# A list scheduler in the kernel sets the order of all five engines in the first mixer of a two-layer decoder trunk

## The chip, the cores and the metric

The kernel runs on one core of a Trainium2 chip. A core has five engines with queues of their own: TensorE (PE in the profile, PEld for its loads of weights), VectorE (DVE), ScalarE (ACT), GpSimd (POOL) and SyncE (SP), which here only starts transfers. Each engine works through its instructions in the order in which the program holds them; semaphores make it wait for the others. The metric is the device time of one execution in microseconds (us), as the median of several runs.

## The reference

The input x has 256 tokens of 2048 channels in fp32. Two layers follow, each a mixer, a gated FFN with a convolution, and a small embedding term. Only the mixer of the first layer, a gated DeltaNet, is touched here:

```python
def gdn_mixer(x, w_in, conv_w, a_log, dt_bias, norm_g, w_o):
    proj = x @ w_in                                   # 2048 -> q 2048, k 2048, v 4096, z 4096, a 32, b 32
    ...
    qkv = silu(causal_dwconv(qkv, conv_w))            # 4 taps along the tokens
    q = l2norm(q) * 128 ** -0.5; k = l2norm(k)        # 16 heads of 128, each used by two of 32 value heads
    beta = sigmoid(b)
    g = -exp(a_log) * softplus(a + dt_bias)
    o = gated_delta_rule(q, k, v, g, beta)
    o = o * rsqrt(mean(o ** 2) + eps) * norm_g * silu(z)
    return o @ w_o                                    # 4096 -> 2048

def gated_delta_rule(q, k, v, g, beta):               # per head; the reference takes chunks of 64 tokens
    ...
    lmat = where(strict, (k * beta) @ k.T * decay, 0)
    sol = triangular_solve(lmat + I, [v * beta, k * beta * exp(gc)])
    ...                                               # scan over chunks: v_new, o_n, state S

x = layer_norm(ALPHA * x + gdn_mixer(x, ...))
```

## The kernel before

**Products.** Every fp32 weight block is 512 KB: SP loads it into a `raw` tile (line 99), ACT writes its upper part `hi` (L103), DVE the rest `lo` = raw − hi (L104); three buffers each. x is kept transposed and split in the same way (`xT`). PE takes x·hi and x·lo in a fast fp32 form. `gemm_t` gives transposed results, 256 columns at a time in two PSUM tiles `mm_ps`: a block is 8 products of 512 columns (L124) and 8 of 256 (L128). `gemm` gives rows, in two tiles `b_ps`: 8 products with hi (L148, L149) and 4 with lo (L152). These PSUM tiles share four buffers (`mm`). The small products of the mixer are plain fp32 and use two buffers `sp` and two buffers `bk`.

**Stages of the mixer.** The 32 value heads are taken as eight groups of four; a group uses two key heads. For each group: keys `k` and queries `q` (256 columns each), values `v` and gates `zs` (512 each), all from `w_in`; keys, queries and values pass through a fold of the two halves of `mm_ps` (L184 on ACT, L185, the join, on DVE), four taps and a tanh. `lower` makes the 256x256 triangle `L` of each head as two diagonal blocks, `l_ps` (L465) by the decay (rows `qd` loaded from the DRAM tile `grow`, L450) by `c` (L472). 32x32 blocks of L go through DRAM (`lt`, then `ld`) to `substitution`, 31 steps on DVE that invert them for four groups at once (`xi`), and back through DRAM (`tt`) into `pm`, which has one buffer (L510, on POOL). `inverses` makes `W` from L and pm (`w_ps`). `front` prepares the decayed score tiles `qd`, `qo`, `n21`. `solve` runs two halves, each pm·rhs and then three products with W, with DVE or ACT between any two (`s_ps`, L504). `outputs` takes `o_ps` (L607, L608), squares (ACT), a reciprocal root on DVE, the scaled tile `ot` (L620), its transposes `ot_ps` (L624) and the split result `oT` (L626, L627). `mixed` multiplies oT of two groups (kt = 8) with w_o and adds to x (L224, L226); the last group's part is done by the following stage (`project`).

**What sets the order.** Emission order by hand in `gdn_groups`, and a scheduler of the framework that places instructions by priority when their operands should be ready. Two devices of the kernel act on it: `hi` and `lo` are emitted with raised priority, and `weights` draws one or two substitution steps per block from the generator `self.aside`. Small products may land anywhere, also in the middle of a block.

Of the kernel before, what the change touches and what calls it, by code (L numbers as in the profile page):

```python
# [57 lines left out]

class Trunk:
    def __init__(self, nc, tc, ctx, t):  # L60
# [21 lines left out]
        self.aside, self.share = iter(()), 0  # L82
# [10 lines left out]
    def weights(self, src, rows, nk, cols):  # L93
# [13 lines left out]
        for _ in range(self.share):  # L107
            next(self.aside, None)
# [196 lines left out]
    def gdn_gates(self, pool, w, gk):  # L305
        nc, t = self.nc, self.t
        ab, dt, al, gr = w[:64, 0:S], w[:, 256:288], w[:, 288:320], w[:64, 320:448]
        self.gemm_t(t["gdn_w_in"], 12288, 64, self.xT, lambda n, ps: self.fold(pool, ab, ps))
        nc.scalar.activation(al, al, AF.Exp)
        ps = self.sp.tile([P, 2, 64], F32, tag="sp", name="ab_ps")  # L310
        for a in range(2):
            nc.tensor.transpose(ps[:, a], ab[:, a * P:(a + 1) * P], self.ident[:64, :64])

        x, e, s, s2, q, g = (
            w[:, o:o + 64].rearrange("p (a h) -> p a h", a=2) for o in range(448, 832, 64))
        nc.vector.tensor_tensor(x, ps[:, :, 0:32], bcast(dt, 2, 1), op=ALU.add)
        nc.vector.scalar_tensor_tensor(e, x, -1.0, x, op0=ALU.mult, op1=ALU.max)
        nc.scalar.activation(e, e, AF.Exp, scale=-1.0)
        nc.vector.tensor_scalar(s, e, 2.0, None, op0=ALU.add)
        nc.vector.reciprocal(s, s)  # L320
        nc.vector.tensor_tensor(s, s, e, op=ALU.mult)
        nc.vector.tensor_tensor(s2, s, s, op=ALU.mult)
        nc.vector.tensor_scalar(q, s2, 1.0 / 17, None, op0=ALU.mult)
        for m in (15, 13, 11, 9, 7, 5, 3):
            nc.vector.scalar_tensor_tensor(q, q, 1.0 / m, s2, op0=ALU.add, op1=ALU.mult)
        nc.vector.scalar_tensor_tensor(q, q, 1.0, s, op0=ALU.add, op1=ALU.mult)
        nc.vector.tensor_scalar(x, x, 0.0, None, op0=ALU.max)
        nc.vector.scalar_tensor_tensor(x, q, 2.0, x, op0=ALU.mult, op1=ALU.add)
        nc.vector.scalar_tensor_tensor(g, x, -1.0, bcast(al, 2, 1), op0=ALU.mult, op1=ALU.mult)

        self.beta = gk.tile([P, 2, 32], F32, tag="beta", name="beta")
        nc.scalar.activation(self.beta, ps[:, :, 32:64], AF.Exp, scale=-1.0)
        nc.vector.tensor_scalar(self.beta, self.beta, 1.0, None, op0=ALU.add)
        nc.vector.reciprocal(self.beta, self.beta)

        self.gc = gk.tile([P, 2, 32], F32, tag="gc", name="gc")
        self.gout = gk.tile([P, 32], F32, tag="go", name="go")
        g64 = g.rearrange("p a h -> p (a h)")
        pc = self.sp.tile([P, 256], F32, tag="sp", name="gc_ps")
        nc.tensor.matmul(pc[:, 0:64], self.tri, g64, start=True, stop=True)  # L340
        nc.tensor.matmul(pc[:, 64:96], self.ones, g[:, 0], start=True, stop=True)
        nc.tensor.matmul(pc[:64, 128:256], g64, self.tri, start=True, stop=True)
        nc.vector.tensor_copy(self.gc.rearrange("p a h -> p (a h)"), pc[:, 0:64])
        self.ngc = gk.tile([P, 2, 32], F32, tag="ngc", name="ngc")
        nc.vector.tensor_scalar(self.ngc, self.gc, -1.0, None, op0=ALU.mult)
        nc.vector.tensor_tensor(self.gout, pc[:, 64:96], self.gc[:, 0], op=ALU.subtract)
        nc.vector.tensor_copy(gr, pc[:64, 128:256])
        self.grow = self.dr.tile([64, P], F32, tag="grow", name="grow", bufs=1)
        nc.gpsimd.dma_start(out=self.grow, in_=gr)

    def gdn(self):
        nc, tc, t = self.nc, self.tc, self.t
        self.op = tc.alloc_tile_pool(name="op", bufs=2)
        with tc.tile_pool(name="gk", bufs=1) as gk, tc.tile_pool(name="gw", bufs=1) as pool:
            cw = gk.tile([P, 4, 64], F32, tag="cw", name="cw")
            ng = gk.tile([P, 1], F32, tag="ng", name="ng")
            cr = pool.tile([64, 4, P], F32, tag="v", name="cr")
            w = pool.tile([P, 1024], F32, tag="xi", name="gates")
            for i, k in enumerate(("gdn_dt_bias", "gdn_a_log")):
                nc.gpsimd.dma_start(out=w[:, 256 + 32 * i:288 + 32 * i],  # L360
                                    in_=bass.AP(tensor=t[k].tensor, offset=t[k].offset, ap=[[0, P], [1, 32]]))
            nc.gpsimd.dma_start(out=cr, in_=t["gdn_conv_w"].rearrange("k (n c) -> n k c", c=P))
            nc.gpsimd.dma_start(out=self.cst, in_=t["cst"][:, P:])
            nc.gpsimd.dma_start(out=ng, in_=t["gdn_norm_g"].rearrange("(p o) -> p o", o=1))
            nc.gpsimd.tensor_scalar(ng, ng, 0.5, None, op0=ALU.mult)

            def load(nb):
                cs = slice(nb * 512, (nb + 1) * 512)
                for a in range(2):
                    nc.sync.dma_start(out=self.x[:, a, cs], in_=t["x"][a * P:(a + 1) * P, cs])  # L370
                for a in range(2):
                    self.to_xT(self.xT, self.x[:, a, cs], a, nb * 4)
                if nb == 2:
                    ps = self.sp.tile([P, 4, 64], F32, tag="sp", name="cw_ps")
                    for k in range(4):
                        nc.tensor.transpose(ps[:, k], cr[:, k], self.ident[:64, :64])
                    nc.vector.tensor_copy(cw, ps)

            self.gdn_groups(pool, gk, cw, ng, load, lambda: self.gdn_gates(pool, w, gk))

    def gdn_groups(self, pool, gk, cw, ng, load, gates):
# [277 lines left out]
        for g in range(8):  # L659
# [13 lines left out]
            if g == 7:  # L673
                mixed(6, 1)
# [311 lines left out]
```

## Time and profile before

| | us |
|---|---|
| median of three runs | 2897.72 |
| the three runs | 2894.42, 2897.72, 2898.40 |
| the profiled execution | 2893.65 |
| its span | 2891.7 |
| its first mixer, up to the projection's first products | 916 |

The profiled execution is a run of its own, 4.1 us under the median; rows of the profile are compared with its time. Its mean granted clock of TensorE is 0.995 of full speed. In the views that follow, a row names a line of the kernel, the engine, and a tile and what it is made from; numbers in brackets behind a row say how long the engine had been idle and what released it. A view by windows gives the busy time of each engine in a stretch, with the number of instructions in round brackets.

### The profile page before, as it was taken

The page shows a single profiled execution, that of the slowest core. Times are in us where ns is not written, and L with a number is a line of the kernel's source. Part 1 is how long each engine was busy: PE and PEld are TensorE (multiplying, and loading weights), DVE is VectorE, ACT ScalarE, POOL GpSimd, SP SyncE. Part 2 cuts the span into 40 slices and gives each one's busy share as a digit, 9 for nine tenths or more (in the row PEclk, how much of TensorE's full clock was granted, in tenths as well). Part 3 has the DMA queues.
Part 4 walks back from the last instruction along what each step waited for, and adds up shares of the span by engine and source line. Part 5 has one row for each costly group of instructions (what it writes and reads, how often), then busy time and mean ns, then how long its engine had stood idle before and what let it go on. Part 6 is the DMA issues. An engine that isn't in the chain of part 4 may idle for free. (4 is left out here: it accounts for less than half of the span.)

```text
span 2891.7 us, 40953 instructions
## 1 busy us (share of the span) xinstructions
PE 2825.3 (98%) x15654; PEld 2432.9 (84%) x15654; DVE 1864.7 (64%) x3007; ACT 1427.1 (49%) x2259; POOL 115.0 (4%) x192
## 2 busy tenths in 40 slices
PE   8999999999999999999999999999999999999998
PEld 6888787788887888888888878888888888888887
DVE  6886668766666766666554665766576666654465
ACT  4755536544543655455433543455365555543353
POOL 0100000000000000000000000110000000000000
PEclk9999999999999999999999999999999999999999
DMA  6665555455554566666655556554556666655555
GB/s 190 197 182 150 153 156 177 148 155 155 164 156 139 168 201 203 193 210 200 199 192 190 186 178 201 172 161 134 194 168 196 194 194 194 195 192 190 193 189 179
DMA packets 415077, 519.70 MB, mean 180 GB/s; under 512 B 19708, under 2 KB 313984, under 8 KB 414880
## 3 DMA queue, kind: packets, MB, share of 16 engines
q1 hardware_dynamic: 407136, 496.76, 54.6%
q0 software_dynamic: 7744, 20.32, 2.9%
q8 instruction: 123, 2.02, 0.3%
q14 instruction: 74, 0.61, 0.1%
HBM read 512.76 MB, written 7.39 MB: 180 GB/s over the span
## 5 line engine op out<-in xcount | busy, mean ns | idle before, releaser
L104 DVE TENSOR_TENSOR lo<-raw,hi 128x1024 fp32r<-128x1024 f32 x925 | 1131.7, 1225 | 791.7 <-ACT hi L103 761.0
L103 ACT ACTIVATE hi<-raw 128x1024 fp32r<-128x1024 f32 x925 | 977.2, 1057 | 1273.0 <-PE b_ps L149 533.6
L124 PE MATMUL mm_ps<-xT,hi 128*128 128x512 f32 (+1 forms) x4176 | 1068.4, 396 | 13.4 <-ACT qd L531 4.7
L124 PEld LDWEIGHTS mm_ps<-xT,hi 128*128 128x128 f32 (+1 forms) x4176 | 750.8, 189 | 148.8 <-ACT qd L531 4.9
L128 PEld LDWEIGHTS mm_ps<-xT,lo 128*128 128x128 f32 (+1 forms) x4176 | 574.0, 190 | 39.9
L128 PE MATMUL mm_ps<-xT,lo 128*128 128x256 f32 (+1 forms) x4176 | 600.1, 284 | 0.0
L148 PE MATMUL b_ps<-hi,xT 128*128 128x512 f32 (+2 forms) x736 | 274.7, 379 | 2.9 <-ACT sg L786 1.7
L149 PE MATMUL b_ps<-hi,xT 128*128 128x512 f32 (+2 forms) x736 | 274.3, 379 | 0.0
L148 PE MATMUL b_ps<-hi,hTA 128*128 128x512 f32 (+1 forms) x640 | 212.4, 347 | 0.0
L149 PE MATMUL b_ps<-hi,hTA 128*128 128x512 f32 (+1 forms) x640 | 212.3, 347 | 0.0
L152 PE MATMUL b_ps<-lo,xT 128*128 128x512 f32 (+2 forms) x736 | 195.7, 383 | 1.9 <-DVE lo L104 1.9
L148 PEld LDWEIGHTS b_ps<-hi,xT 128*128 128x128 f32 x736 | 139.0, 189 | 29.5 <-ACT sg L786 3.0
L149 PEld LDWEIGHTS b_ps<-hi,xT 128*128 128x128 f32 x736 | 139.3, 190 | 24.7
L152 PEld LDWEIGHTS b_ps<-lo,xT 128*128 128x128 f32 x736 | 130.8, 189 | 25.1 <-DVE lo L104 2.8
L152 PE MATMUL b_ps<-lo,hTA 128*128 128x512 f32 (+1 forms) x640 | 138.6, 347 | 0.0
L149 PEld LDWEIGHTS b_ps<-hi,hTA 128*128 128x128 f32 x640 | 121.2, 189 | 15.0
L148 PEld LDWEIGHTS b_ps<-hi,hTA 128*128 128x128 f32 x640 | 121.2, 189 | 14.9
L152 PEld LDWEIGHTS b_ps<-lo,hTA 128*128 128x128 f32 x640 | 105.1, 189 | 15.0
L148 PE MATMUL b_ps<-hi,oT 128*128 128x512 f32 (+1 forms) x264 | 101.7, 389 | 0.0
L149 PE MATMUL b_ps<-hi,oT 128*128 128x512 f32 (+1 forms) x264 | 101.4, 386 | 0.0
L408 DVE SCALAR_TENSOR_TENSOR ac<-pd,cw,ac 128x256 f32<-128x256 f32 x192 | 86.3, 479 | 4.6 <-ACT ac L406 4.2
L725 DVE SCALAR_TENSOR_TENSOR fac<-fpd,fcw,fac 128x256 f32<-128x256 f32 x160 | 77.3, 483 | 12.9 <-ACT fac L723 10.0
(265 smaller groups left out, 2351.5 us busy)
## 6 DMA issues: line engine op xcount, KB each, us to landing
raw<-in_gdn_w_in SPq DMA_DIRECT2D x193, 512.0 KB, 3.8
raw<-in_ffn_w_gate SPq DMA_DIRECT2D x160, 512.0 KB, 4.6
raw<-in_ffn_w_up SPq DMA_DIRECT2D x160, 512.0 KB, 4.2
raw<-in_ffn_w_down SPq DMA_DIRECT2D x160, 512.0 KB, 3.6
raw<-in_dsa_w_in SPq DMA_DIRECT2D x80, 512.0 KB, 3.5
raw<-in_gdn_w_o SPq DMA_DIRECT2D x64, 512.0 KB, 3.6
raw<-in_ple_w_gate SPq DMA_DIRECT2D x64, 512.0 KB, 3.7
raw<-in_dsa_w_o SPq DMA_DIRECT2D x32, 512.0 KB, 3.5
```

The lines of the kernel that those rows point to most:

```text
L103: nc.scalar.activation(hi, raw, AF.Copy)
L104: ins = nc.vector.tensor_tensor(lo, raw, hi.bitcast(F32), op=ALU.subtract)
L124: nc.tensor.matmul(q[:m, :], hi[:, k, o:o + m], x[:, k0 + k].rearrange("p a b -> p (a b)"), start=k0 + k == 0, stop=False)
L128: nc.tensor.matmul(q[:m, S:], lo[:, k, o:o + m], x[:, k0 + k, 0, :], start=False, stop=k0 + k == kt - 1)
L148: nc.tensor.matmul(ps[a][:, :n], xh, hi[:, k, :], start=k0 + k == 0, stop=False)
L149: nc.tensor.matmul(ps[a][:, :n], xl, hi[:, k, :], start=False, stop=False)
L152: self.last = nc.tensor.matmul(ps[a][:, :n], x(k0 + k)[:, 0, a * P:(a + 1) * P], lo[:, k, :], start=False, stop=k0 + k == kt - 1)
L408: nc.vector.scalar_tensor_tensor(ac, pd[:, k:k + S], w[:, k:k + 1], ac, op0=ALU.mult, op1=ALU.add)
L725: nc.vector.scalar_tensor_tensor(ac, pd[:, k:k + S], cw[:, k, n:n + 1], ac, op0=ALU.mult, op1=ALU.add)
```

## The change

The mixer is written as tasks, each with an engine, a duration in us (a constant in the code), an emitting function, tasks that come before it, and the buffers it takes and gives back (`raw`, `mm`, `sp`, `qd`, `pm`, ...). `Plan.run` simulates the five engines and the transfers with these numbers, picks at each step the task that can start first (among those that could start now, the lowest rank), and emits it. The whole is put into the program under a manual schedule for all five engines, so the framework's scheduler no longer moves anything there. The blocks of weights have a fixed order on PE (`run`, `merge`); every small product is a task between two half blocks. The rest of the program is unchanged, except that in this stage's last blocks the projection's first hi and lo are mixed in.

```diff
+class Plan:
+    LAG = {"PE": 0.6, "DVE": 0.25, "ACT": 0.25, "POOL": 0.2, "SP": 0.2}
...
+    def run(self):
+        while True:
+            best = None
+            for engine, tasks in self.open.items():
+                pick, at = None, self.at[engine]
+                for t in tasks:
+                    s = self.start(t)
+                    if s is None:
+                        continue
+                    key = (s if s > at + 0.05 else 0.0, t.rank(), t.order)
+                    if pick is None or key < pick[0]:
+                        pick = key, s, t
+                if pick and (best is None or pick[1] < best[1]):
+                    best = pick
...
+            self.at[t.engine] = s + t.cost
+            t.end = s + t.cost + t.tail
...
+            for n in t.then:
+                n.left -= 1
+                n.ready = max(n.ready, t.end + (n.lag if n.engine != t.engine or t.tail else 0.0))
...
+            with tc.manual_schedule(engines=engines):
+                self.gdn_plan(pool, gk)
...
+        plan = self.plan = Plan(raw=3, hi=3, lo=3, mm=4, sp=2, bk=2, fold=2, pd=2, ac=2, k=6, q=1, v=2, vt=1, zs=2, oT=2,
+                                qd=2, qo=2, n21=2, sq=1, L=5, pm=1, W=1, u=1, y0=1, y=2, wq=2)
...
+            urgent = lambda: 0 if i <= plan.now + 1 else 3
...
+            d = add(Q, 0.38, load, take=["raw"], rank=i, bus=2.2, tail=1.8)
+            h = add(A, 1.06, high, [d], take=["hi"], rank=urgent)
+            l = add(V, 1.23, low, [h], take=["lo"], give=["raw"], rank=urgent)
...
+            p = add(E, b["cost"][0], lambda: product(0), deps, take=["mm"] * 2 * b["first"], rank=5, lag=0.1)
+            p = b["task"] = add(E, b["cost"][1], lambda: product(1), [l, p], give=["hi", "lo"], rank=4, lag=0.1)
...
+            d = add(Q, 0.4, lambda: rows_into(g, tile()), [rows["go"]], take=[take], rank=lambda: plan.now + 2.5, bus=2.2, tail=3.5)
...
+                    p = add(V, 0.69, lambda scale=scale: scale((0, 1)), [p, dec[g][a], d], rank=5 if b else 3)
...
+                d = add(V, 0.36 + 0.0028 * m * n, step, [d, z], rank=5 if b else 3.5)
...
+                ld.append(add(G, 0.6, fill, [s["t"], *ld[:1]], take=["pm"] * (not c), tail=3.5))
...
-            lT = pool.tile([P, 32, 32], F32, tag="u", name="lT")
-            nc.vector.tensor_copy(lT, ld.rearrange("p i j -> p j i"))
...
-            if g in (2, 4, 6):
-                mixed(g - 2, 2)
...
+        run([x for y in zip(keys(0), keys(1)) for x in y])
+        run(column(w_in, 0, 12288, 64, KT, lambda k: self.xT[:, k], True, None, decay_gates))
+        run(keys(2))
+        run(keys(3))
+        batch(0)
+        run(gates(0))
+        run(merge(queries(0) + values(0), gates(1)))
...
+        for g in range(1, 7):
+            c = queries(1) if g == 1 else []
+            c = c + values(g)
+            if g < 3:
+                c = c + keys(2 * g + 2) + keys(2 * g + 3)
+            if g == 6:
+                c = c + values(7)
+            c = c + queries(g + 1)
+            z = gates(g + 1)
+            if g < 6:
+                z = z + mixes(g - 1)
+            run(merge(c, z))
...
+        run(mixes(5))
+        run(mixes(6))
+        plan.run()
```

Work that differs: `mixes` takes one group at a time (kt = 4), so x is added to 56 times in place of 32; L is scaled inside its own tile, which the decay rows are loaded into; the substitution reads `ld` with a stride in place of a transposed copy; `outputs` writes over `zs` in place of `ot`; the sums of squares of the keys go through four small instructions per batch in place of one. The numbers of products on PE and of transfers are the same.

The first place is DVE while the first four groups' L are scaled (`L<-l_ps,c,L`); `pd<-mm_ps,fold` is the join that frees a PSUM tile of the wide products. Before:

```order
L104 TENSOR_TENSOR lo<-raw,hi 128x1024
L472 SCALAR_TENSOR_TENSOR L<-l_ps,c,L 128x128 x8
L104 TENSOR_TENSOR lo<-raw,hi 128x1024
L472 SCALAR_TENSOR_TENSOR L<-l_ps,c,L 128x128 x7
L104 TENSOR_TENSOR lo<-raw,hi 128x1024
L472 SCALAR_TENSOR_TENSOR L<-l_ps,c,L 128x128 x6
L104 TENSOR_TENSOR lo<-raw,hi 128x1024
L472 SCALAR_TENSOR_TENSOR L<-l_ps,c,L 128x128 x6
L185 TENSOR_TENSOR pd_109<-mm_ps,fold 128x256
L185 TENSOR_TENSOR pd_110<-mm_ps,fold 128x256
```

The same place after (L515 is lo, L845 the scaling, L548 the join, L623 the swish of the z gate):

```order
L845 SCALAR_TENSOR_TENSOR L<-l_ps,c,L 128x128 x6
L515 TENSOR_TENSOR lo<-raw,hi 128x1024
L623 SCALAR_TENSOR_TENSOR zs<-zs,b_ps 128x512
L845 SCALAR_TENSOR_TENSOR L<-l_ps,c,L 128x128 x2
L515 TENSOR_TENSOR lo<-raw,hi 128x1024
L623 SCALAR_TENSOR_TENSOR zs<-zs,b_ps 128x512
L845 SCALAR_TENSOR_TENSOR L<-l_ps,c,L 128x128 x2
L515 TENSOR_TENSOR lo<-raw,hi 128x1024
L845 SCALAR_TENSOR_TENSOR L<-l_ps,c,L 128x128 x2
L515 TENSOR_TENSOR lo<-raw,hi 128x1024
L845 SCALAR_TENSOR_TENSOR L<-l_ps,c,L 128x128 x4
L515 TENSOR_TENSOR lo<-raw,hi 128x1024
```

Scalings stand in runs of 6 to 8 between two lo before, and in runs of 2 to 6 after; the z gate, which needs no join, is done here, and the next joins (`pd`) come after the last scaling and one more lo.

The second place is the end of the mixer on DVE: the last reciprocal root `rs`, the scaled outputs of the last group, and their split transposes `oT`. Before:

```order
L251 SCALAR_TENSOR_TENSOR rs_8261<-rt_8262,rs_8261 128x8
L620 SCALAR_TENSOR_TENSOR ot<-o_ps,rs_8261,zs 128x128 x8
L627 SCALAR_TENSOR_TENSOR oT<-ot_ps,ng,oT 128x4x128 x2
L104 TENSOR_TENSOR lo<-raw,hi 128x1024 x2
L224 TENSOR_TENSOR x<-x,b_ps 128x512
```

And after (L1045 is the scaling, L303 a residual addition, L185 a lo of the projection, L1061 the split):

```order
L1045 SCALAR_TENSOR_TENSOR zs<-o_ps,rs_8235,zs 128x128 x2
L515 TENSOR_TENSOR lo<-raw,hi 128x1024
L303 TENSOR_TENSOR x<-x,b_ps 128x512 x2
L515 TENSOR_TENSOR lo<-raw,hi 128x1024
L1045 SCALAR_TENSOR_TENSOR zs<-o_ps,rs_8235,zs 128x128 x4
L515 TENSOR_TENSOR lo<-raw,hi 128x1024
L303 TENSOR_TENSOR x<-x,b_ps 128x512
L185 TENSOR_TENSOR lo<-raw,hi 128x1024
L303 TENSOR_TENSOR x<-x,b_ps 128x512
L1045 SCALAR_TENSOR_TENSOR zs<-o_ps,rs_8235,zs 128x128 x2
L185 TENSOR_TENSOR lo<-raw,hi 128x1024
L1061 SCALAR_TENSOR_TENSOR oT<-ot_ps,ng,oT 128x4x128
```

Before, the eight scalings and the two splits follow each other with no weights between; now five lo and the additions of other blocks stand among them.

The third place is PE in the first groups' solve: wide products (`mm_ps`) and small ones (`s_ps`, `w_ps`, `ss_ps`). Before:

```order
L124 MATMUL mm_ps<-xT,hi 128x512 x2
L504 MATMUL s_ps<-vt,pm 128x128
L124 MATMUL mm_ps<-xT,hi 128x512 x5
L504 MATMUL s_ps<-vt,pm 128x128
L124 MATMUL mm_ps<-xT,hi 128x512
L504 MATMUL s_ps<-vt,pm 128x128 x2
L128 MATMUL mm_ps<-xT,lo 128x256 x8
L124 MATMUL mm_ps<-xT,hi 128x512
L504 MATMUL s_ps<-y_2228,W 128x128 x4
L124 MATMUL mm_ps<-xT,hi 128x512 x4
L504 MATMUL s_ps<-y,W 128x128 x4
L124 MATMUL mm_ps<-xT,hi 128x512 x3
```

After (L478 and L475 are the wide products with hi and lo, L916 the small products of the solve, L772 sums of squares):

```order
L478 MATMUL mm_ps<-xT,hi 128x512 x8
L916 MATMUL w_ps<-pm,L 128x96 x8
L475 MATMUL mm_ps<-xT,lo 128x256 x8
L916 MATMUL s_ps<-vt,pm 128x128 x4
L478 MATMUL mm_ps<-xT,hi 128x512 x8
L772 MATMUL ss_ps<-cst,sq 128x1 x4
L916 MATMUL s_ps<-y_1960,W 128x128 x4
L475 MATMUL mm_ps<-xT,lo 128x256 x8
```

Small products split half blocks before; after, they stand whole between two halves.

More of the change, by code (lines that the diff above doesn't have):

```diff
@@ L302, in layer_norm @@
         return affine
[L305 to L349, printed above, removed]
@@ L359, in gdn @@
[L359 to L364, printed above, removed]
@@ L365, in gdn @@
[L365 to L377, printed above, removed]
@@ new lines, in mixes, with done @@
+        def mixes(g):
+            r = []
+            for nb in range(4):
+                c = nb * 512
+                def done(state, task, c=c, nb=nb):
+                    for a in range(2):
+                        add(V, 0.69, lambda a=a: self.residual(self.x[:, a, c:c + 512], state["ps"][a], None,
+                                                               1.0 if g else ALPHA),
+                            [task], give=["mm"] + ["oT"] * (nb == 3 and a), rank=1)
+                r += column(t["gdn_w_o"], 4 * g * P, c, 512, 4, lambda k: O[g]()[:, k], False, lambda k0: od[g], done)
+            return r
@@ new lines, in merge, with run @@
+        def merge(a, b):
+            pairs = [b[i:i + 2] for i in range(0, len(b), 2)]
+            n, j, r = len(a) // 4, 0, []
+            for i in range(n):
+                k = len(pairs) * (i + 1) // n
+                mine, j = pairs[j:k], k
+                mid = mine[:1] if len(mine) > 1 else []
+                r += a[4 * i:4 * i + 2] + sum(mid, []) + a[4 * i + 2:4 * i + 4] + sum(mine[len(mid):], [])
+            return r
+        def run(blocks):
+            for b in blocks:
+                place(b)
@@ new lines, in squares, with sq, product @@
+        def squares(y, deps, use, take=()):
+            box = {}
+            def sq():
+                box["sq"] = new("sq", [2, S])
+                nc.scalar.activation(box["sq"], y(), AF.Square)
+            def product():
+                ps = box["ps"] = sps("sp", [4], "ss_ps")
+                for h in range(2):
+                    for a in range(2):
+                        nc.tensor.matmul(ps[:, 2 * h + a:][:, 0:1], box["sq"][:, h, a * P:(a + 1) * P],
+                                         self.ones[:, 0:1], start=True, stop=True)
+            d = add(A, 0.63, sq, deps, take=["sq"], rank=3)
+            d = add(E, 0.7, product, [d], take=["sp"], give=["sq"], rank=1)
+            return add(V, 0.17, lambda: use(box["ps"]), [d], take=take, give=["sp"], rank=2)
@@ new lines, in gdn_plan, with taps @@
+        add(Q, 0.4, lambda: None, bus=0.6)
+        tb0 = {}
+        def taps():
+            ps = tb0["ps"] = sps("sp", [4, 64], "cw_ps")
+            for k in range(4):
+                nc.tensor.transpose(ps[:, k], cr[:, k], self.ident[:64, :64])
+        quarter(0)
+        tapped = add(E, 0.3, taps, [there], take=["sp"], rank=1)
+        tapped = add(V, 0.4, lambda: nc.vector.tensor_copy(cw, tb0["ps"]), [tapped], give=["sp", "u"], rank=1)
+        for nb in range(1, 4):
+            quarter(nb)
@@ L677, in gdn_groups @@
             if g == 1:
[L678 to L679 removed]
+                front(1)
             if g == 2:
[L681 to L683 removed]
+                batch(1)
+            group(g)
+            front(g + 1)
+        group(7)
+        run(mixes(5))
+        run(mixes(6))
+        plan.run()
+        self.heads[7] = O[7]()
     def project(self, pool, src, h, kt, g, b, prepare, side=1, scale=ALPHA):
```

807 lines of the change are left out of this document (556 added, 251 removed).

## The prediction

> **What bounds the kernel now.** I read the first page of the profile, then a table by stage, then what PE waits for in the first mixer, then the timeline around the longest of those waits.
>
> ```profile
> span 2891.7 us, 40953 instructions
> PE 2825.3 (98%) x15654; PEld 2432.9 (84%) x15654; DVE 1864.7 (64%) x3007; ACT 1427.1 (49%) x2259; POOL 115.0 (4%) x192
> ```
>
> PE is busy for 98% of the span and no other engine for more than 64%, apart from the weight loads, which overlap PE. So the time can only fall by less idle PE, a higher granted clock, or less work on PE. The next rows are the first mixer and the stage behind it: microseconds, then busy time and count of PE, PEld, DVE, ACT and POOL, granted clock, DMA share, GB/s.
>
> ```profile
> 0.00:916.00 916.00, 871.47 (x4875) 741.97 (x4875) 638.49 (x1222) 473.84 (x904) 47.43 (x87) 0.99 0.56 164
> 916.00:1740.00 824.00, 817.07 (x4489) 707.18 (x4489) 517.80 (x705) 403.25 (x558) 25.89 (x47) 1.00 0.61 192
> ```
>
> The mixer leaves PE idle for 916.00 − 871.47 = 44.5 us; the next stage, of nearly the same length, for 6.9. All that a better order can win lies in those 44.5 us, in the clock lost behind them, and in what PE itself pays for the order of its products. The waits of PE from the start to 935 us (waiting instruction, releaser, us in total, times, longest):
>
> ```profile
> PE ot_ps L624 <- DVE ot L620: 10.8, 8, 4.5
> PE v_ps L563 <- DVE v L411: 6.3, 3, 5.2
> PE t_ps L195 <- DMA x<-in_x: 5.8, 2, 4.9
> PE mm_ps L124 <- ACT qd L531: 4.7, 1, 4.7
> PE l_ps L465 <- DVE oT L627: 3.3, 2, 2.0
> PE mm_ps L124 <- DVE xT L189: 3.3, 2, 1.8
> PE mm_ps L124 <- ACT hi L103: 2.9, 1, 2.9
> PE t_ps L195 <- DVE xT L189: 1.8, 1, 1.8
> PE s_ps L504 <- DVE y L595: 1.6, 2, 0.9
> PE b_ps L148 <- DVE pd L185: 1.2, 1, 1.2
> PE s_ps L504 <- DVE vt L587: 1.0, 1, 1.0
> PE s_ps L504 <- ACT y L590: 0.7, 1, 0.7
> PE kk_ps L425 <- ACT sq L422: 0.4, 1, 0.4
> ```
>
> They add up to 43.8 us, the idle time of the stage. Three single waits (4.5, 5.2, 4.7) make a third of it. Their causes:
>
> ```profile
> 105.03 1.22 DVE L104 TENSOR_TENSOR lo<-raw,hi 128x1024 fp32r<-128x1024 f32 x1 [1.32 <-ACT hi L103]
> 106.17 1.64 DVE L472 SCALAR_TENSOR_TENSOR L<-l_ps,c,L 128x128 f32<-128x128 f32 x6
> 107.73 0.74 DVE L185 TENSOR_TENSOR pd<-mm_ps,fold 128x256 f32<-128x256 f32 x2
> 108.28 1.19 PE L124 MATMUL mm_ps<-xT,hi 128*128 128x512 f32 x2 [4.72 <-ACT qd L531]
> 457.98 0.69 ACT L528 ACTIVATE qo<-qd,go 128x128 f32<-128x128 f32 x2 [4.35 <-DMA qd<-grow]
> 459.66 1.23 DVE L104 TENSOR_TENSOR lo<-raw,hi 128x1024 fp32r<-128x1024 f32 x1 [3.34 <-ACT hi L103]
> 463.97 1.12 PE L563 MATMUL v_ps<-ident,v 128*128 128x128 f32 x4 [5.15 <-DVE v L411]
> 909.52 0.39 PE L608 MATMUL o_ps<-u,qd 128*128 128x128 f32 x2
> 914.37 0.97 PE L624 MATMUL ot_ps<-ident,ot 128*128 128x128 f32 x3 [4.46 <-DVE ot L620]
> ```
>
> At 108 us the named releaser, ACT's qd, is not the real one. PE needs an mm buffer, and the two DVE joins that free it (L185) begin at 107.73, behind six scalings of L and a weight split that nobody is waiting for yet. At 458 us ACT stands 4.35 us at the head of its queue for a transfer (qd from grow); the next hi half, the convolution and PE follow late. At 914 us PE has nothing left beside the last group: its o_ps products end at about 910, and squares, rsqrt and scaling must pass before the transposes.
>
> **Clock.** The same columns as above, for the stretch behind each of these waits, for a stretch after recovery, and for one with short waits:
>
> ```profile
> 108.20:113.00 4.80, 4.71 (x15) 4.05 (x16) 3.88 (x11) 4.80 (x15) 2.55 (x5) 0.52 0.50 149
> 463.70:469.00 5.30, 5.03 (x17) 4.12 (x17) 3.85 (x8) 3.56 (x9) 0.00 (x0) 0.61 0.72 224
> 914.30:919.00 4.70, 4.63 (x14) 2.81 (x15) 3.32 (x10) 1.37 (x2) 1.02 (x2) 0.64 0.00 0
> 113.00:117.00 4.00, 4.00 (x30) 3.69 (x28) 3.06 (x7) 3.91 (x10) 0.33 (x1) 1.00 0.59 180
> 521.00:527.00 6.00, 4.41 (x29) 3.64 (x27) 3.81 (x8) 1.44 (x2) 0.56 (x1) 1.00 0.73 229
> ```
>
> Each long wait is followed by about five microseconds at a granted clock of 0.52 to 0.64. At 521 to 527 us PE idles 1.6 us in shorter pieces and the clock stays at 1.00.
>
> **The change, part by part.**
>
> *Long waits.* Whatever frees an mm buffer on DVE (join, swish, addition) now carries rank 1 and the scalings of L rank 3; at this place the z gate's blocks run, and their swish stands between short runs of scalings. The decays' rows are loaded by a rank among the weights and their ACT pieces, cut to two heads each, carry rank 4, so hi halves don't stand behind them. In the tail, five blocks of other products stand between the last o_ps and the last transposes; a block lasts 2.80 us by the chain of waits in steady running:
>
> ```profile
> 1773.75 1.84 PE mm_ps L124 x8
> 1776.55 1.84 PE mm_ps L124 x8
> ```
>
> Five blocks are 14.0 us, against the 4.9 us from 909.52 to 914.37 that the chain took. I count all three as gone: 4.72 + 5.15 + 4.46 = −14.3.
>
> *Clock behind them.* 4.8 × 0.48 + 5.3 × 0.39 + 4.7 × 0.36 = 2.3 + 2.1 + 1.7 = −6.1, work that then runs at full speed. The Trainium skill, "TensorE: Matmul & The Clock Gate", section "HAM oscillation — how this bites in real kernels", puts it as half clock for a window of about 3.4 us after any idle gap of that length; the trace agrees on which waits do it, and an estimate from that page, three times 1.7 us, would make this term −5.1 instead.
>
> *Head.* The first x (4.9), the rest of that row (0.9), the first hi (2.9) and the two rows on xT (3.3, 1.8) are 13.8. What waits for the first transfers cannot go: 4.9 + 2.9. The remaining 6.0 hangs on transposes, splits and joins in a queue that is now ordered by rank; I take half, −3.0.
>
> *Other waits.* 43.8 − 14.3 − 13.8 = 15.7, in 17 pieces of at most 2.0 us. The planner sends a dependent task at least 0.6 us after a PE task in its own count, so most should go, but it also makes new places: some 160 groups of small products (v 16, w 8, s 72, o 16, ot 16, l 8, g 8, squares 16) now stand at fixed spots between half blocks, each ready or not by its own jitter. I take 12 us of waits left, old and new: −3.7. Ends: nothing left, −15.7, and more than before (first rival).
>
> *PE's own order.* Small fp32 products no longer split a half block; changes from small to large products fall from 196 to 133. What such a change costs is seen at the starts here:
>
> ```profile
> 892.21 0.40 PE L148 MATMUL b_ps<-hi,oT 128*128 128x512 f32 x1
> 892.44 0.40 PE L149 MATMUL b_ps<-hi,oT 128*128 128x512 f32 x1
> 892.76 1.16 PE L504 MATMUL s_ps<-y,W 128*128 128x128 f32 x8
> ```
>
> From large to large 0.23, from large to small 0.32: 0.09 us more. 63 × 0.09 = −5.7. If the way back costs as much it is −11.3; if the next group swallows it, nothing.
>
> *More additions on DVE.* w_o is now taken one group at a time, which adds 24 residual additions; the two copies that transposed L go, which I count as nothing.
>
> ```profile
> L104 DVE TENSOR_TENSOR lo<-raw,hi 128x1024 fp32r<-128x1024 f32 x252 | 308.4, 1224 | 166.8 <-ACT hi L103 145.3 <-ACT ac L406 6.9 <-ACT y L590 6.5
> L224 DVE TENSOR_TENSOR x<-x,b_ps 128x512 f32<-128x512 f32 x24 | 16.3, 682 | 8.2 <-PE b_ps L152 8.2
> ```
>
> 24 × 0.682 = 16.4 us: DVE goes from 638 to 655 of some 883 us, 74%. They lie beside PE's products: the sum has 0 for them. Covered by DVE's idle time, 167 us of it in front of lo alone. Without that cover each addition would hold an mm buffer for 0.7 us longer; at worst the whole 16.4 comes onto the path. PE's product counts are unchanged, so nothing for those. The small tensor_scalars, four per batch in place of one, are covered likewise.
>
> *Seam.* The loads of the first layer norm's rows on POOL are moved behind other loads that wait for the same last oT, and their use lies tens of microseconds later: 0.
>
> *Sum.* −14.3 − 6.1 − 3.0 − 3.7 − 5.7 = −32.8. The profiled execution took 2893.65 us, so 2860.9 by its account. It lies 4.1 below the median of the three runs before and 0.8 below the fastest; half of the 4.1 added gives **2863**.
>
> **Rivals.**
>
> 1. *The plan has no slack where the chip has jitter.* Every engine runs in a fixed order, and a late transfer or a long DVE piece holds all behind it. For it: ACT's 4.35 us above is such a case. Against it: three raw buffers and 167 us of DVE idling on hi. At 0.1 us for each of 160 groups that is 16 us more waits: −17, so about **2878**.
>
> 2. *Slower: the reload of pm.* It has one buffer, written by four POOL transfers per group, which must wait for the last read of the group before. In the new order the first w_ps of a group stands 2.6 to 3.0 blocks behind that read in five places, so 7.3 to 8.4 us.
>
> ```profile
> L510 POOL DMA_DIRECT2D pm<-tt x32: 582/582/616, 177.2 to 828.6; - x32
> pm<-tt POOLq DMA_DIRECT2D x32, 32.0 KB, 2.4
> ```
>
> Four issues are 4 × 0.58 = 2.3 us, and the landing has a median of 2.4 (last column), so it fits by about 3 us. If landing took 13 us there, each of five waits would be 2.3 + 13 − 7.8 = 7.5 us and cost 2.0 in clock: +47, so **2908**. It decides for slower from 6.6 us each on (32.8 / 5), a landing of about 10 us. Against it: that is four times the median.
>
> 3. *Slower: the clock.* With small groups at every half block PE may idle briefly all the time, and the granted clock could swing without one long wait. At 0.80 over the some 245 us in which solves and outputs run (8 groups × 11 blocks × 2.80), 61 us are lost: **2922**. The 521 us row speaks against it: 1.6 us idle of 6, clock 1.00. The Trainium skill, same page, section "A second HAM failure mode: psum-queue depth-cycling", says that PE idling for a moment between groups of matmuls is enough to make the clock swing; by that rule this rival would come about, and the trace so far does not bear it out.
>
> 4. *No gain.* The waits named above are replaced by others of the same sum and the switches cost nothing: **2897**.
>
> **How the numbers follow.** The forecast, between −25 and −45 (2850 to 2870 with the 2 us for the runs): 0.62. Its lower end is the sum with all middle waits gone, −44.8; its upper end is the sum without the terms for switches and other waits, rounded up. Rival 1, 2870 to 2890: 0.20. No gain: 0.08. Rival 2: 0.06, rival 3: 0.04. What can be told from no change is about 0.2%, 5.8 us, so 2892 to 2903. The range 2850 to 2890 takes the forecast and rival 1, 0.82. Faster 0.82, same 0.08, slower 0.10.
>
> **What would show it.** In the profile after: PE waits of the first mixer of 20 to 25 us in all, with the first x (4.9) the longest; no stretch under 0.9 in granted clock behind the first 20 us; no single wait above 3 us behind the head; the stage's end, the first products of the projection, some 30 us earlier than 916, near 883; DVE busy in the stage up by about 15; the later 1975 us unchanged within a few. Wrong: w_ps waiting for pm on POOL (rival 2), a clock between 0.6 and 0.9 over tens of microseconds in groups (rival 3), many waits of 0.3 to 1 us on s_ps or ss_ps (rival 1). A time below 2850 would mean that switches cost PE both ways.

## The result and the profile after

The changed kernel takes 2851.93 us in the median of four runs (2850.62 to 2857.97); the kernel before, 2896.56 in the median of its four. The ratio is 0.985, 95% interval 0.9833 to 0.9867: 44.6 us or 1.5% less. The forecast was 2863 with 2850 to 2890. The profiled execution of the changed kernel is the slowest of its four, 2857.97 us.

The first page, and the mixer up to the transposes of the next stage's column vectors (`col_ps`), which begin at 928.7 us before and at 888.3 after. The window's columns are microseconds, busy time and count of PE, PEld, DVE, ACT, POOL, granted clock, DMA share, GB/s. Before:

```profile
0.00:928.70 928.70, 884.17 (x4925) 751.45 (x4925) 645.44 (x1230) 478.88 (x909) 52.81 (x99) 0.99 0.55 163
```

After:

```profile
span 2855.9 us, 40967 instructions
PE 2811.6 (98%) x15654; PEld 2438.0 (85%) x15654; DVE 1898.3 (66%) x3035; ACT 1428.2 (50%) x2259; POOL 115.2 (4%) x192
...
0.00:888.30 888.30, 869.28 (x4924) 755.16 (x4924) 678.69 (x1258) 479.61 (x909) 52.92 (x99) 0.99 0.59 170
```

The stage is 40.4 us shorter: PE's idle time fell by 25.5 us (44.5 to 19.0) and its busy time by 14.9, with the same products. The rest of the program is 4.6 us longer in this one execution (1967.6 against 1963.0); in the profiles of all other kernels here it takes 1962.8 to 1966.0. What PE waits for in the stage after (us in total, times, longest):

```profile
PE t_ps L446 <- DMA x<-in_x: 5.7, 1, 5.7
PE b_ps L485 <- DVE pd L548: 4.3, 2, 2.9
PE mm_ps L478 <- ACT hi L511: 3.2, 1, 3.2
PE mm_ps L478 <- DVE zs L623: 2.7, 2, 1.4
PE b_ps L485 <- ACT hi L511: 2.0, 1, 2.0
PE b_ps L483 <- DVE lo L515: 0.6, 1, 0.6
PE mm_ps L478 <- DVE xT L451: 0.5, 1, 0.5
```

No small product waits behind the first x any more: there is no row for v, s, ot, l or w. The two rows on DVE, pd and zs (7.0 us), are waits for buffers of the wide products; before, there was 1.2 us on pd and no row on zs. They lie between 160 and 181 us:

```profile
174.93 0.22 DVE L874 TENSOR_TENSOR xi<-xi,xt 128x31 f32<-128x31 f32 x1
175.06 0.48 DVE L555 SCALAR_TENSOR_TENSOR ac<-pd,cw,ac 128x256 f32<-128x256 f32 x1
175.78 1.23 DVE L515 TENSOR_TENSOR lo<-raw,hi 128x1024 fp32r<-128x1024 f32 x1 [0.24 <-ACT hi L511]
176.92 1.00 DVE L555 SCALAR_TENSOR_TENSOR ac<-pd,cw,ac 128x256 f32<-128x256 f32 x2
177.96 0.42 DVE L548 TENSOR_TENSOR pd<-mm_ps,fold 128x256 f32<-128x256 f32 x1
178.53 0.47 PE L485 MATMUL b_ps<-hi,xT 128*128 128x512 f32 x1 [2.92 <-DVE pd L548]
```

The substitution of the first batch (the first four groups) ends at 175 us; only then do the convolution's taps (`ac`) get DVE, then the join, and PE has stood for 2.9 us. Windows of the same kernel around the two places, then two long stretches:

```profile
161.00:167.00 6.00, 4.67 (x16) 3.69 (x17) 5.73 (x12) 0.81 (x1) 0.00 (x0) 0.72 0.39 122
178.50:184.00 5.50, 4.07 (x12) 3.01 (x13) 5.32 (x14) 2.59 (x6) 2.36 (x4) 0.63 0.54 146
500.00:600.00 100.00, 100.00 (x556) 86.68 (x556) 90.17 (x168) 53.33 (x98) 0.56 (x1) 1.00 0.58 170
600.00:700.00 100.00, 100.00 (x577) 87.55 (x576) 69.36 (x115) 49.65 (x94) 4.69 (x8) 1.00 0.56 162
```

At the new waits the clock falls as it did at the old ones (0.52 to 0.64 there). From 500 to 700 us PE is never idle, but DVE is busy for 90 of the first 100 us.

### The profile page after: what moved, and what is told of

Read it like the earlier page. It is cut to its first block, busy times and chain, and to the rows that moved or that the text cites. A ratio compares the mean times of both kernels' runs of the same rounds, so it can differ in the third digit from the quotient of the medians.

```text
span 2855.9 us, 40967 instructions
## 1 busy us (share of the span) xinstructions
PE 2811.6 (98%) x15654; PEld 2438.0 (85%) x15654; DVE 1898.3 (66%) x3035; ACT 1428.2 (50%) x2259; POOL 115.2 (4%) x192
## 5 line engine op out<-in xcount | busy, mean ns | idle before, releaser
L185 DVE TENSOR_TENSOR lo<-raw,hi 128x1024 fp32r<-128x1024 f32 (+1 forms) x676 | 827.2, 1225 | 627.9 <-ACT hi L184 618.9
L184 ACT ACTIVATE hi<-raw 128x1024 fp32r<-128x1024 f32 (+1 forms) x676 | 714.0, 1056 | 932.7 <-PE b_ps L228 398.8
L203 PE MATMUL mm_ps<-xT,hi 128*128 128x512 f32 x3136 | 791.6, 393 | 2.9 <-DVE rs L324 1.5
L203 PEld LDWEIGHTS mm_ps<-xT,hi 128*128 128x128 f32 x3136 | 564.4, 189 | 104.5 <-issue 2.3
L207 PE MATMUL mm_ps<-xT,lo 128*128 128x256 f32 x3136 | 447.0, 284 | 0.0
L511 ACT ACTIVATE hi<-raw 128x1024 fp32r<-128x1024 f32 x249 | 262.9, 1057 | 212.5 <-PE mm_ps L478 105.9
L515 DVE TENSOR_TENSOR lo<-raw,hi 128x1024 fp32r<-128x1024 f32 x249 | 303.8, 1222 | 73.4 <-ACT hi L511 68.4
L478 PE MATMUL mm_ps<-xT,hi 128*128 128x512 f32 (+1 forms) x1040 | 264.9, 397 | 6.4 <-ACT hi L511 3.2
L478 PEld LDWEIGHTS mm_ps<-xT,hi 128*128 128x128 f32 (+1 forms) x1040 | 190.3, 190 | 45.0 <-ACT hi L511 3.6
L475 PE MATMUL mm_ps<-xT,lo 128*128 128x256 f32 (+1 forms) x1040 | 148.9, 286 | 0.0
L475 PEld LDWEIGHTS mm_ps<-xT,lo 128*128 128x128 f32 (+1 forms) x1040 | 138.9, 190 | 7.2 <-issue 0.2
L228 PEld LDWEIGHTS b_ps<-hi,hTA 128*128 128x128 f32 x640 | 121.2, 189 | 14.9
```

The lines of the kernel that those rows point to most:

```text
L184: nc.scalar.activation(hi, raw, AF.Copy)
L185: ins = nc.vector.tensor_tensor(lo, raw, hi.bitcast(F32), op=ALU.subtract)
L203: nc.tensor.matmul(q[:m, :], hi[:, k, o:o + m], x[:, k0 + k].rearrange("p a b -> p (a b)"), start=k0 + k == 0, stop=False)
L207: nc.tensor.matmul(q[:m, S:], lo[:, k, o:o + m], x[:, k0 + k, 0, :], start=False, stop=k0 + k == kt - 1)
L228: nc.tensor.matmul(ps[a][:, :n], xl, hi[:, k, :], start=False, stop=False)
L475: nc.tensor.matmul(ps[o][:m, S:], lo[:, k, o * P:o * P + m], x(k0 + k)[:, 0], start=False, stop=e)
```

## Experiments

Each kernel is the changed one with the edit shown, unless it says otherwise. Time is the median of its runs; the changed kernel, run again beside the next three, took 2851.81 us (ratio 0.9851, 0.9838 to 0.9865).

**The changed kernel again** (a_same).

> The changed kernel itself, once more, as the base for the others and as a second look at what differs from run to run. In the first profile PE busy fell by 14.9 us and PE's waits by 25.5 us up to the projection's column transposes (928.7 to 888.3 us). Theory: the waits at 160 us (swish, 2.7) and 178 us (joins, 4.3) are in the order and come back; waits of the mixer again 17 to 21 us, time 2850 to 2858. Rival: they are chance of one execution; then waits of 10 us or so here.

Its waits on pd and zs are 4.3 and 2.7 us again, and all waits together 18.5: these two belong to the order, not to one execution. The clock does not repeat as well: here the wait for hi at 82 us (2.4, against 2.0) is followed by a granted clock of 0.52 from 82 to 89 us, which the first profile does not have.

**As many changes between small and large products as before** (a_split).

```diff
 def mul(lhs, rhs, ps):
-    for h in h4: nc.tensor.matmul(ps[:, h], lhs[:, h], rhs[:, h], ...)
+    part((0, 1))
+    plan.late = plan.cur, lambda: part((2, 3))   # put behind the first two products of the next half block
```

> The changed kernel, but of 88 groups of four small products each the last two are put behind the first two products of the next half block: 197 changes from small to large products instead of 133, as many as before; all else as planned. Theory: a change costs PE about 0.09 us on the way in and 0.09 on the way back, so 64 x 0.18 = +11.5 us against the changed kernel, in PE busy and not in waits. First rival: it costs one way only, +5.8. Second rival: it is free and the fall in PE busy came from the clock: within 2 us.

2850.98 us, 0.8 less than the changed kernel: the second rival's time. PE in the stage:

```profile
0.00:885.40 885.40, 868.10 (x4925) 753.26 (x4925) 676.92 (x1258) 478.40 (x909) 52.83 (x99) 1.00 0.58 171
```

64 more changes, and PE busy is 1.2 us lower. The clock is not what hides a cost: with the time lost at half clock taken off (worked out under "Clock" in the next section), PE busy is 864.8 here and 864.5 and 862.9 in the two profiles of the changed kernel, so at most 2 us more, against the 5.8 and 11.5 expected. A change of product kind costs nothing that can be seen. The row on which I had put 0.09 us (892.76, s_ps 0.32 us behind the product ahead) reads otherwise with DVE's row beside it, from before:

```profile
892.02 0.69 DVE L595 TENSOR_TENSOR y<-y,s_ps 128x512 f32<-128x512 f32 x1 [0.21 <-PE s_ps L504]
```

y ends at 892.71, the product that needs it starts at 892.76. PE waited for y, too short a time to be listed as idle.

**Longer substitution steps in the plan** (a_slack).

```diff
-d = add(V, 0.36 + 0.0028 * m * n, step, [d, z], rank=5 if b else 3.5)
+d = add(V, 0.50 + 0.0034 * m * n, step, [d, z], rank=5 if b else 3.5)
```

> The changed kernel, with each of the substitution's steps entered in the plan as longer than it is (0.50 + 0.0034 per element in place of 0.36 + 0.0028; the batch of 31 then counts 37.5 us in place of 26). Theory: DVE has no slack in the plan while the substitution runs, falls behind, and the swish and the joins that free PSUM come late; with slack the waits at 160 and 178 us and the low clock behind them go: 6 to 10 us faster than the changed kernel. Rival: those waits have another cause (a transfer, ACT) or the substitution's later end makes a new wait for pm: no faster, or slower by up to 5.

2866.13 us, 14 more than the changed kernel: my theory of these waits was wrong. The wait at 178 us grew from 2.9 to 8.0:

```profile
PE b_ps L485 <- DVE pd L548: 8.9, 2, 8.0
```

The taps carry rank 3.8, the steps 3.5. A join has rank 1, but it needs a pad buffer, and both are held by taps that wait behind the steps. Longer steps keep them there longer. It is a rank turned round by a buffer, not a want of slack.

That is not all of the 14 us. The second substitution ends at 630 us here, 595 in the changed kernel, and 6.5 us of new waits of PE lie between 678 and 693 us, in the solves that stand behind it.

**The three long waits alone, in the kernel before** (b_three).

```diff
 def fold(...):
+    with self.tc.high_priority(offset=W_AHEAD):   # fold and join
-dm = pool.tile(..., tag="qd", name="qd", bufs=2)
+dm = pool.tile(..., tag="qd", name="qd", bufs=3)
-L = Ls[g] = pool.tile(..., name="L", bufs=6)
+L = Ls[g] = pool.tile(..., name="L", bufs=5)
-if g == 7: mixed(6, 1)
 outputs(g, f, u, zs)
+if g == 7: mixed(6, 1)
```

> The kernel before, no planner, with three small edits against its three long waits: joins at the priority of the weights' halves, a third qd buffer (room for it from a sixth L buffer), and the last group's outputs emitted ahead of the last w_o products. Theory: each wait goes with the clock loss behind it, 14.3 + 6.1 = 20 us faster than before, half of what the planner gains. Rival one: the three waits were nearly everything, 30 us or more. Rival two: the framework's scheduler makes new waits in their place, under 10 us.

2875.85 us against 2894.96 beside it, ratio 0.9929 (0.9917 to 0.9942): 19.1 us, the size that the theory gave. So 43% of the gain needs no planner. PE in the stage, two of its waits, and the stretch behind the second of them:

```profile
0.00:911.10 911.10, 883.27 (x4925) 754.01 (x4925) 643.15 (x1230) 478.00 (x909) 52.87 (x99) 0.99 0.57 166
...
PE v_ps L564 <- DVE v L412: 2.6, 3, 1.6
PE kk_ps L426 <- ACT sq L423: 2.5, 1, 2.5
...
88.40:96.00 7.60, 7.60 (x31) 7.04 (x32) 3.73 (x17) 3.89 (x11) 0.00 (x0) 0.55 0.74 179
```

The sum is made up otherwise than the theory said. The stage is 17.6 us shorter, 16.7 of it idle time: two of the three long waits are gone and the third is 1.6. PE busy stays where it was (883 against 884), so the clock's 6.1 did not come back: kk_ps, which waited 0.4 us before, waits 2.5 and is followed by a clock of 0.55, and six short waits of s_ps between 511 and 522 us (4.2 together) by 0.53 from 515 to 526. That 19.1 is so near to 20 is in part luck.

**L transposed by ACT for the first batch** (a_lT).

```diff
+lT = lazy(lambda: new("u", [32, 32]))
+if not b:
+    d = add(A, 1.0, lambda: nc.scalar.activation(lT(), ld().rearrange("p i j -> p j i"), AF.Copy), [d], take=["u"], rank=1)
-... bcast(ld()[:, i + 1:, i], m, 1) ...
+... bcast(ld()[:, i + 1:, i] if b else lT()[:, i, i + 1:], m, 1) ...
-d = add(V, 0.36 + 0.0028 * m * n, ...)
+d = add(V, 0.36 + (0.0028 if b else 0.002) * m * n, ...)
```

> The changed kernel, with the first batch's L blocks transposed once by ACT (into u, which is free until the first solve) so that the substitution reads rows again, and its steps entered as shorter in the plan (0.0020 per element). In the changed kernel the step's first instruction takes 469 ns on average with the strided read, 341 before: 31 x 128 = 4.0 us of DVE in the stretch from 130 to 190 us, where DVE is busy 55 of 60 us. Theory: DVE is the bound there, the convolution's taps stand behind the steps, the buffers behind them fill and PE waits for swish and joins (2.7 + 4.3 us, then half clock); with 4.0 us less the waits shrink by about as much: 3 to 6 us faster than the changed kernel. Rival: the waits come from the order alone (taps ranked behind steps) whatever the steps take: within 1.5 us.

2847.13 us (2845.57 to 2848.23), ratio 0.9833 (0.982 to 0.9845): 4.7 us less than the changed kernel, within the theory. The rows of the step's first instruction, in the stage, before, after and (from 100 to 200 us) in this kernel:

```profile
L495 DVE TENSOR_TENSOR xt<-lT,xi 128x31 f32<-128x31 f32 (+15 forms) x62 | 21.1, 340 | 1.1
```

```profile
L872 DVE TENSOR_TENSOR xt<-ld,xi 128x31 f32<-128x31 f32 (+15 forms) x62 | 29.1, 469 | 1.3 <-DMA ld<-lt 0.4
```

```profile
L877 DVE TENSOR_TENSOR xt<-u,xi 128x31 f32<-128x31 f32 (+15 forms) x31 | 10.5, 339 | 3.3 <-ACT u L868 2.8
```

The strided read of the changed kernel cost 0.13 us in each of 62 instructions, 8.0 us, for the 2.3 us of copies that the change saved. The row on pd is gone; the swish still waits (3.6 us).

**No slack for the small products** (a_jit).

```diff
-LAG = {"PE": 0.6, "DVE": 0.25, "ACT": 0.25, "POOL": 0.2, "SP": 0.2}
+LAG = {"PE": 0.0, "DVE": 0.0, "ACT": 0.0, "POOL": 0.0, "SP": 0.0}
+if engine == "PE" and lag is None: cost *= 0.45
```

> The changed kernel, planned without slack for the small products: all lags 0 and the small products entered at 0.45 of their cost, so that they stand right behind what they need. In the trace of before 153 of 195 entries into small products come less than 0.5 us after their operand, with 85 ns more than the usual step in the median of the freshest; after, 4 of 132. Theory: what PE busy lost (14.9 us) is this price of fresh operands, paid at entries and between groups, and not a change of product kinds: PE busy up by 8 to 15 us here, and more short waits: 15 to 30 us slower than the changed kernel. Rival: entries are free and only waits over a few tenths count: PE busy within 3 us, 0 to 8 us slower.

2880.23 us, 28 more, PE busy 880.0 in the stage (10.7 more): the size is the theory's, the mechanism only half. Entries whose operand ended 60 to 200 ns ahead cost no more than others here (20 of 131, medians of −1.5 and −0.5 ns against the usual step). A fresh operand has no price; being late has. And a large part of the 28 us is another matter: the second substitution ends at 652 us, and the solves behind it stand without products between (next but one experiment). PE waits 16.3 us more than in the changed kernel, and 11.2 us of its waits lie between 667 and 702 us, in these solves; and of the 10.7 us of busy time, half (5.3) is time lost at half clock.

**One duration for all** (a_flat).

```diff
+if engine in ("DVE", "ACT"): cost = 0.8
```

> The changed kernel, planned with one duration, 0.8 us, for every task on DVE and ACT in place of the measured ones (lo counts 0.8 for 1.2, the last substitution steps 0.8 for 0.4). Theory: the plan needs the durations where DVE is full and in the tail (there only 0 blocks are left between the last o_ps and ot_ps in its order): tail wait of about 4.5 us with 1.7 of clock back, more waits up to 190 us: 10 to 25 us slower than the changed kernel. Rival: order and ranks do the work, durations hardly matter: within 4 us.

2896.0 us in twelve runs, ratio 0.9998 (0.999 to 1.0007): far more than the theory, the whole gain. Its largest waits:

```profile
PE mm_ps L480 <- DVE pd L550: 9.2, 3, 4.6
PE mm_ps L480 <- DVE zs L625: 8.9, 2, 7.3
PE t_ps L448 <- DMA x<-in_x: 6.1, 2, 4.6
PE w_ps L918 <- DVE zs L1047: 5.1, 1, 5.1
PE ot_ps L1056 <- DVE zs L1047: 4.3, 1, 4.3
```

The tail wait is back (4.3), joins and swish are late, and a w_ps waits for an earlier group's outputs (5.1). The second substitution is late here too (649 us): 9.4 us of the waits lie between 689 and 711 us. PE is idle for 49.2 us of the stage, as against 19.0, and most of the rest is clock.

**56 more instructions on DVE** (a_add).

```diff
 self.residual(xb, state["ps"][a], None, 1.0 if g else ALPHA)
+nc.vector.tensor_tensor(xb, xb, xb, op=ALU.max)      # cost in the plan 1.38 for 0.69
```

> The changed kernel, with each of its 56 residual additions followed by one more DVE instruction on the same tile (x = max(x, x), some 0.68 us, known to the plan): 38 us more DVE, against the 16.4 us that the change added. Theory: behind 190 us they lie beside PE's products: 0 to 3 us for them, but the last blocks are fuller, and in this order the last transposes stand right behind the last o_ps block at the end, so up to 6 us for the tail. Rival: DVE is near its bound in the later groups too; then 10 us or more, and the 24 additions were not free.

2881.21 us, 29 more: the rival's time. The tail costs 3.7 of it; the rest begins in the middle. POOL's store behind the second substitution, after and here, and two stretches here:

```profile
595.47 0.56 POOL L876 DMA_DIRECT2D tt<-xi  x1 [113.17 <-DVE xi L874]
```

```profile
646.44 0.56 POOL L879 DMA_DIRECT2D tt<-xi  x1 [160.33 <-DVE xi L877]
...
500.00:600.00 100.00, 100.00 (x556) 86.72 (x555) 91.53 (x165) 53.59 (x98) 0.00 (x0) 1.00 0.56 168
600.00:700.00 100.00, 87.33 (x476) 75.78 (x475) 68.45 (x130) 43.00 (x86) 5.25 (x9) 0.95 0.47 134
...
690.33 2.02 PE L919 MATMUL w_ps<-pm,L 128*128 128x96 f32 x8 [5.09 <-DVE zs L1048]
```

The second substitution has the lowest rank and takes what DVE has left. With 38 us more work it ends 51 us later; group 4's solve must wait for it, the blocks meant to stand between the solves have been used up, and PE idles for 12.7 of 100 us. The same deadline was missed in a_slack, a_jit and a_flat.

**The same, with the second batch ranked ahead** (a_add_b1).

```diff
-rank=5 if b else 3      (scalings of L)      -rank=5 if b else 3.5   (steps)
+rank=3                                       +rank=3.5
```

> The changed kernel with 56 more DVE instructions on x, which cost 29 us, and now the second batch's scalings and substitution at the first batch's ranks (3 and 3.5 in place of 5). With the 56 instructions the second substitution ended at 645 us (594 without), the first w_ps of group 4 moved from 612 to 660, and PE ran three solves without products between them. Theory: the 29 us come from that deadline, since the second substitution takes only what DVE has left; ranked ahead, it ends in time and 15 to 25 us come back (2856 to 2866). Rival: DVE is short in every group, so joins and additions now come late instead: 2875 or more.

2888.11 us, 7 more still: again the rival. The last step now starts at 538 us, but the joins are late:

```profile
PE b_ps L485 <- DVE pd L548: 9.6, 4, 4.3
PE mm_ps L478 <- DVE pd L548: 8.0, 2, 5.2
```

Ranks only choose who waits: with this load it is DVE that PE waits for in the middle of the stage, whichever work comes first.

**Without the 24 additions** (a_less).

```diff
+out = g in (1, 3, 5)          # this part of the output is left out
-add(V, 0.69, lambda a=a: self.residual(...), [task], ...)
+add(V, 0.01 if out else 0.69, (lambda: None) if out else lambda a=a: self.residual(...), [task], ...)
```

> The changed kernel without the residual additions of groups 1, 3 and 5 (24 instructions; this part of the output is left out), so that DVE does 16.4 us less, about what it did before. Theory: the 24 additions that the change brought lay beside PE's products: within 2 us of the changed kernel. Rival: DVE was already short between 400 and 650 us (82 and 90% busy), and the additions cost some of it: 4 us or more faster.

2851.83 us, the changed kernel's time to 0.1 us: the 24 additions cost nothing that can be seen.

**Taps ahead of steps when no pad is free, and slower row loads in the plan** (c_pdrows; on top of a_lT).

```diff
-step, [d, z], rank=5 if b else 3.5
+step, [d, z], rank=5 if b else (lambda: 3.5 if plan.room["pd"] else 3.9)
-rank=lambda: plan.now + 2.5, bus=2.2, tail=3.5      (loads of decay rows)
+rank=lambda: plan.now + 2.5, bus=3.2, tail=5.0
```

> The kernel with L transposed by ACT (2847.1 us, against 2851.9 of the changed one), and two more edits of the plan: the first batch's substitution steps rank ahead of the convolution's taps only while a pad buffer is free (else 3.9 against 3.8), and the loads of decay rows are entered as slower (bus 3.2, landing 5.0; landings of 11.5 us were seen where six of them follow each other at 80 us). Theory: the waits at 160 to 163 us (swish, 3.6 in all) and at 80 us (hi, 1.9) go, with half clock behind the first: 4 to 8 us faster than that kernel, so 2839 to 2843. Rival: the substitution is the bound of the first solve whatever its rank; it ends later, the solves of the first two groups stand without products between them, and the time is the same or up to 10 us more.

2844.81 us (2843.01 to 2846.72), ratio to the kernel before 0.9824 (0.9811 to 0.9837): the lowest median of all, 7.1 us under the changed kernel and 2.3 under a_lT, where the theory had 4 to 8. The runs of the two overlap (a_lT's begin at 2845.57), so the 2.3 is hardly clear of noise, and which of the two edits brought what was not told apart. Its stage and its longest waits:

```profile
0.00:878.40 878.40, 864.68 (x4925) 751.55 (x4925) 673.41 (x1258) 481.08 (x910) 52.74 (x99) 1.00 0.60 172
...
PE t_ps L446 <- DMA x<-in_x: 5.7, 2, 5.4
PE mm_ps L478 <- ACT hi L511: 4.4, 2, 2.6
PE b_ps L485 <- ACT hi L511: 2.7, 3, 1.5
```

PE waits for DVE's pd and zs no more, and behind the start the clock is 1.00 throughout. ACT's hi is now late in five places (7.1 us, the first one at the start among them; 5.2 in the changed kernel), which is where a part of the theory's gain went.

## Why the prediction was right, and where not

- **What bounds.** Right: the gain lies in the mixer (its stage is 40.4 us shorter in the profiles), in idle PE and in what hides in its busy time. The two profiled executions differ by 35.7 us only, since the rest of the program was 4.6 longer in the second; the first lies 2.9 under its median and the second 6.0 over its, which makes the 44.6. The 4.2 by which this exceeds the stage is not explained by these profiles.
- **Sum.** Of −32.8, −21.0 was to be idle time (long waits, head, other waits) and −11.8 busy time (clock, PE's own order). Idle time fell by 25.5, by the mechanisms named. Busy time fell by 14.9, but neither of its two terms holds, as the next points show: that the sum still came near is luck.
- **Three long waits.** Right, −14.3: none of the three is left in the changed kernel.
- **Clock.** Mis-sized: −6.1 was taken for good, but the new waits bring new stretches of half clock. These are all of them in the stage behind the first 17 us, three before and two after (the record of the clock begins at 14 to 16 us; until then each kernel starts slowly, with 0.43 us from one large product to the next):

```profile
106.00:112.80 6.80, 4.51 (x13) 3.85 (x14) 5.88 (x19) 6.80 (x22) 2.39 (x6) 0.50 0.65 201
461.00:467.80 6.80, 3.83 (x11) 3.18 (x12) 5.35 (x11) 6.00 (x14) 0.57 (x1) 0.50 0.71 230
914.90:918.30 3.40, 3.40 (x11) 1.91 (x10) 2.11 (x7) 1.37 (x2) 0.32 (x1) 0.50 0.00 0
...
162.90:166.30 3.40, 3.40 (x9) 2.73 (x10) 3.16 (x8) 0.11 (x1) 0.00 (x0) 0.50 0.53 154
180.00:186.80 6.80, 6.17 (x17) 4.93 (x18) 5.80 (x16) 4.11 (x11) 2.36 (x4) 0.50 0.25 75
```

  PE was busy for 11.7 us of them before and for 9.6 after. Half of that is lost, 5.9 and 4.8, so the term came to −1.1; in the changed kernel's second profile, with the stretch at 82 us, 8.0 were lost, and nothing was gained. In the kernel without the new waits (c_pdrows) there is no such stretch, and the term comes out whole. The Trainium skill, "TensorE: Matmul & The Clock Gate", section "HAM oscillation — how this bites in real kernels", ties the fall to an idle gap of about 3.4 us. The trace does not agree: 1.45 and 1.23 us with one product between them were followed by 0.72.
- **Head.** −3.0 was said; 13.8 became 5.7 + 3.2 + 0.5 = 9.4, so −4.4.
- **Other waits.** 12 us left were said, 9.6 are there (7.0 on joins and swish, 2.0 on hi, 0.6 on lo), so −6.1 for −3.7. That PE's plan lag would clear the small products' waits was right; that what is left would be jitter was wrong, the largest two rows came back in the second profile and are in the order.
- **PE's own order.** This is the step that failed. −5.7 for 63 changes of product kind rested on a row that was a wait for y, and a_split put 64 changes back at no cost. With the time lost in these stretches of half clock taken off, PE busy was 878.3 us before and is 864.5 after; reckoned in the same way it is 875.9 in b_three, 864.8 in a_split, 866.0 in a_flat and 864.7 in c_pdrows. So nearly all of the 14.9 comes with the planner's order, neither from the clock nor from the changes. Where it lies can be worked out from the starts of PE's rows. The time from a large product to the next large one across small products, less the large one's usual step, was 192.2 us in 195 runs of small products before and is 145.0 in 132 after, with 1348 small products in each. Of these 47.2 us, 30.4 are listed waits inside the runs, all of them gone, and 16.8 are not listed. Half clock is about 1 of the 16.8: PE was busy at half clock for 3.0 us inside these runs before and is for 1.1 after. The rest is waits too short to be listed: outside the half clock, 119 steps of these runs began less than 0.1 us after their operand was released and took 9.4 us more than usual steps, where after 32 such steps take 0.2 more. A run of eight had a median of 0.900 us and has 0.816. Between large products the stage lost 6.8 (25.6 to 32.4): the new waits. 47.2 − 6.8 = 40.4. So the gain is that small products find their operands there.
- **DVE's additions.** Free, as said (a_less). But DVE's busy time in the stage rose by 33.2 us (645.4 to 678.7) where about 15 was said: the additions are 16.4, the strided reads 8.0, the copies −2.3, and some 11 are not accounted for. The words "the two copies that transposed L go, which I count as nothing" left out what reads them: 62 instructions became 0.13 us longer, and mending that for one batch, in the kernel and in its plan, brought 4.7 us. And 74% on average was the wrong number for the cover: DVE had 90% from 500 to 600 us, and 38 us more work cost 29.
- **Seam and pm.** No wait on either: the rival of pm did not come, nor the one of a clock that swings over tens of microseconds. But the sign "no stretch under 0.9" failed (0.72 and 0.63). The rival without slack did not come in the changed kernel; with the slack taken out (a_jit) the plan loses 28 us, much of it by the late second substitution.

## What to carry to other kernels

A list scheduler is worth what its durations are worth: with one flat value the whole gain was gone. Its own waits come from ranks that meet at a shared buffer (a join of rank 1 behind taps of rank 3.8), so look at who holds the buffer. Read a short interval on the bounding engine together with the producer's end on the other engine before it is given a price of its own. The cover for added work is the busiest stretch, not the mean, and work of lowest rank has a deadline: see when it ends and who starts on it. Four of the edits tried here made the second substitution 34 to 56 us late.

## What the hardware showed that I had not expected

PE's granted clock fell to 0.72 and 0.63 behind pairs of waits of 1.45 and 1.23, and of 2.92 and 1.40 us, each with one or a few products between. In the kernel before only longer single waits had shown it, and 1.6 us of idling in 6 had not (521 to 527 us). Later runs show it behind single waits of 2.4 us (0.52 over 7 us, a_same) and 2.5 us (0.55 over 7.6 us, b_three). A DVE instruction of 255 elements that reads one operand with a stride of 32 took 620 ns in the first batch (611 over both), 425 with rows.
